# Sixteen experts of unequal load on one core: tiles of one or two experts replaced by tiles of up to four, in equal column strips

## The chip, the cores and the metric

The kernel runs on one core of a Trainium2 chip. The metric is the device time of one execution in microseconds (us); lower is better. Engines are named as in the profile: PE (TensorE, with PEld for its weight loads), DVE (VectorE), ACT (ScalarE), POOL (GpSimd) and SP (SyncE, which here issues the weight loads).

## What is computed

A two-layer backbone over 256 latent and 256 context tokens of width 1024. Each layer first mixes tokens in four branches (a recurrence, a long convolution, a short convolution, attention), merges them and normalises; none of that is touched. Then follows a mixture of 16 experts of which every token uses two. Layer 0 routes all 512 tokens, layer 1 the 256 latent ones:

```python
def moe(h, router_w, router_bias, w1, w3, w2):
    ...
    wts = jnp.take_along_axis(s, idx, axis=-1)
    wts = wts / jnp.sum(wts, -1, keepdims=True)
    gates = jnp.einsum('nk,nke->ne', wts, jax.nn.one_hot(idx, N_EXPERTS, dtype=F32)).astype(h.dtype)
    out = jnp.zeros_like(hf)
    for e in range(N_EXPERTS):
        act = jax.nn.silu(hf @ w1[e]) * (hf @ w3[e])
        out = out + gates[:, e:e + 1] * (act @ w2[e])
    return out.reshape(B, T, D)
```

Per expert w1 and w3 are 1024 x 512 and w2 is 512 x 1024, all fp32: 2 MB each, 6 MB an expert, 96 MB a layer.

## The kernel before

**Places and tiles.** The function `moe` routes, counts the tokens of each expert, and sorts the experts by count into 16 places; place 0 and place 1 always hold experts 0 and 1, so that their weights can be loaded before routing is known. A tile is 128 rows, one row for each token-expert pair, and `ROOM` says how many rows a place owns. `WORK` lists groups as (first place, experts, tiles). A group is one expert in one, two or three tiles of its own, or two neighbouring experts that share one tile, 64 columns each.

**One group.** `expert_in` (L1413) multiplies the tile's 128 gathered tokens by w1 and w3: the tokens are the stationary operand, w1 and w3 move through, 8 blocks of 128 rows each. Where two experts share a tile, each has 64 columns of the stationary operand, so that its output stands on its own 64 partitions. ACT and DVE form silu(.) times the other half (L1425), PE transposes that (L1429), and `expert_out` (L1445) multiplies by w2, whose result ACT writes out to `yd`. For the next group, PE finds the token numbers with 128x1 matmuls (L1543), the tokens are gathered by DMA, and PE turns them (L1560); layer 1 gathers by matmuls instead. `places` is the DVE operation that makes a tile's choice matrix.

**Weights.** A load is half of one matrix, 1 MB, 4 of its 8 row blocks for w1 and w3, 2 of 4 for w2. All 96 loads of a layer go out in order on SP's queue: those of experts 0 and 1 from L371, the others from L1691 with an expert number that SP has read first (L1702). They fill a ring of 11 buffers in layer 0 and 13 in layer 1, so that load i is issued when the matmuls on load i-11 (or i-13) are done.

**Room that runs out.** Where an expert has more tokens than its rows, a loop at the end (`For_i`, L1724) takes 128 of them a turn, of one expert, with loads of its own; `NOV` is the most turns that the layer may need, and the part of `yd` for them is set to zero at the program's start by DMAs from POOL (L1788).

**Counts.** The reference's routing of its drawn inputs gives, by place, in layer 0: 68 51 260 169 87 71 64 56 34 31 28 27 25 20 19 14 tokens; in layer 1: 46 38 65 55 44 41 32 30 28 26 23 22 18 17 16 11.

Of the kernel before, what the change touches and what calls it, by code (L numbers as in the profile page):

```python
# [34 lines left out]

ROOM = ([128, 128, 384, 256, 128, 128] + [64] * 10, [64, 64, 128, 128] + [64] * 12)
# [30 lines left out]
def host_constants():  # L67

    f = np.float32
    cols = {}  # L70
# [62 lines left out]
    for l in range(DEPTH):  # L133
        cols[f"room{l}"] = np.broadcast_to(np.array(ROOM[l], f), (128, 16))
        cols[f"base{l}"] = np.broadcast_to((np.cumsum(ROOM[l]) - ROOM[l]).astype(f), (128, 16))
    early = ("win", "zT", "iota", "lead", "token", "room0", "base0", "room1", "base1")
# [29 lines left out]
def backbone(ctx: ExitStack, tc: tile.TileContext, a: dict, out: bass.AP, dbg=None):  # L166
# [1234 lines left out]

    def expert_in(xs, w1, w3, n):


        W = 128 // n
# [29 lines left out]

    def expert_out(aa, w2, n, ydst):

        W = 128 // n
        py = [[xbank(), xbank()] for _ in aa]
        for k in range(4):  # L1440
            for h in range(2):
                for x in range(n):
                    c = slice(W * x, W * x + W)
                    for p, t in zip(py, aa):
                        PE.matmul(p[h][c, :], t[:, k, c], w2[x](k)[:, h * 512:h * 512 + 512], start=(k == 0),  # L1445
                                  stop=(k == 3), skip_group_check=n > 1)
        for p, d in zip(py, ydst):
            aas["y"] = aas.get("y", 0) + 1
            yo = wt("y1", [128, 1024]) if aas["y"] % 2 else unit("R7")[:, :1024]
            for h in range(2):  # L1450
                ACT.activation(yo[:, h * 512:h * 512 + 512], p[h], AF.Copy)  # L1451
            ACT.dma_start(d, yo)

    def moe(l, hh, hl, s, nt, crit, closing):
# [70 lines left out]
        DVE.scalar_tensor_tensor(qp, qv, 1.0, oh, op0=OP.add, op1=OP.mult)  # L1525
        work = WORK[l]
        xu = [0, None, 0]
# [26 lines left out]
        def turned(t, dst):  # L1554
# [7 lines left out]
            return dst  # L1562

        def chosen_rows(g, queue):
            p0, n, tiles = work[g]
            out = []
            if xu[2] % 2:
                xu[2] += 1
            for j in range(tiles):
                P = wt("y0", [128, 1024])[:, j % 2 * 512:j % 2 * 512 + nt * 128]  # L1570
                P = P.rearrange("p (i t) -> p i t", i=nt)
                qj = queue[:, :, p0:p0 + n]
                if j:
                    qj = wt("m_rq", [128, 2, 4, 2], bufs=1)[:, 0, :nt, :1]
                    DVE.tensor_scalar(qj, queue[:, :, p0:p0 + 1], -128.0 * j, None, op0=OP.add)
                marks.append(places(P, iota, qj, nt, n, 128 // n).ins)
                out.append(rows_of(P))
            return out

        def inputs(g, queue):  # L1580

            p0, n, tiles = work[g]
            out = []
            for j, dst in enumerate(room_for(tiles)):
                P = wt("y0", [128, 1024], F32R)[:, j % 2 * 512:j % 2 * 512 + nt * 128]
                P = P.rearrange("p (i t) -> p i t", i=nt)
                qj = queue[:, :, p0:p0 + n]
                if j:
                    qj = wt("m_rq", [128, 2, 4, 2], bufs=1)[:, 0, :nt, :1]
                    DVE.tensor_scalar(qj, queue[:, :, p0:p0 + 1], -128.0 * j, None, op0=OP.add)  # L1590
                marks.append(places(P, iota, qj, nt, n, 128 // n).ins)
                out.append(gather(P, hh, hl, dst))
            return out

        marks = list(crit)
        direct = nt == 2
        if direct:
            xs = inputs(0, qp)
        else:
            xs = [turned(t, d) for t, d in zip(chosen_rows(0, qp), room_for(work[0][2]))]  # L1600
        first = list(marks)
# [93 lines left out]
        def fetch(w, es):  # L1695

            hs = [[half(w, e, x) for e in es] for x in range(2)]
            per = D * DE // a[w].shape[3] // 256
            return [lambda k, j=j: hs[k // per][j](k) for j in range(len(es))]
# [4 lines left out]
        starts = [sum(ROOM[l][:p]) for p in range(16)]  # L1704
        for g, (p0, n, tiles) in enumerate(work):
            es = [p if p < 2 else expert(p) for p in range(p0, p0 + n)]
            queue = qs if g + 1 < len(work) and work[g + 1][0] > 1 else qp
            if not direct and g + 1 < len(work):
                rows = chosen_rows(g + 1, queue)
            with ExitStack() as order:  # L1710
                if g == 0:
                    for mk in first:
                        order.enter_context(tc.issue_after(mk))
                aa = expert_in(xs, fetch("exp_w1", es), fetch("exp_w3", es), n)
            if g + 1 < len(work):
                if direct:
                    xs = inputs(g + 1, queue)
                else:
                    xs = [turned(t, d) for t, d in zip(rows, room_for(work[g + 1][2]))]
            expert_out(aa, fetch("exp_w2", es), n,  # L1720
                       [yd[starts[p0] + 128 * j:starts[p0] + 128 * j + 128, :] for j in range(tiles)])
        closing()

        with tc.For_i(0, nc.values_load(ni[0:1, 0:1], min_val=0, max_val=NOV[l]), 1) as jv:  # L1724
            ev = SP.value_load(exi[0:1, ds(jv + 16, 1)], min_val=0, max_val=NE - 1)
            rg["tags"], rg["n"] = ("R0", "R1", "R9", "TZ", "R2", "cv0"), 0
            ws = [fetch(w, [ev]) for w in ("exp_w1", "exp_w3", "exp_w2")]
            P = wt("y0", [128, 1024], F32R if direct else F32)[:, :nt * 128].rearrange("p (i t) -> p i t", i=nt)
# [6 lines left out]
            dst = room_for(1)[0]  # L1735
            aa = expert_in([gather(P, hh, hl, dst) if direct else turned(rows_of(P), dst)], ws[0], ws[1], 1)
            expert_out(aa, ws[2], 1, [yd[ds(jv * 128 + XB, 128), :]])
        rg["tags"], rg["n"] = ("ring",), 0
# [222 lines left out]
```

## Time and profile before

| | |
|---|---|
| median of three runs | 1873.0 us (1869.58 to 1877.13) |
| the profiled execution's own time | 1867.61 us |
| its span | 1865.5 us |
| PE busy | 1665.6 us, 89% of the span |
| DVE, ACT, POOL busy | 46%, 30%, 6% |
| mean DMA rate | 206 GB/s over the span |
| experts of layer 0 on PE | 729.0 to 1075.9 us |
| experts of layer 1 on PE | 1579.4 to 1829.7 us |

The span is the time from the first to the last instruction; the execution's own time lies 2.1 us above it. PE's share is an average over the whole program. The two expert stages, which the change touches, are read apart from the rest, in windows and in the timeline.

### The profile page before, as it was taken

Reading aid. Unit: us, or ns where it says so; the run is one execution under the profiler, and the core shown is the slowest. Engines: PE = TensorE matmul, PEld = TensorE weight load, DVE = VectorE, ACT = ScalarE, POOL = GpSimd, SP = SyncE. Lnnn points to the kernel's source line nnn. Section 1 sums busy time; section 2 is a strip of 40 time slices with the busy share of each in tenths; the row PEclk is TensorE's granted clock in tenths of the full one; section 3 lists DMA queues with packets and bytes.
Section 4 is the critical chain, followed back from the end, with each engine's and each line's share of the span. In section 5 each row is a group of like instructions: output and inputs, shape, how many; then the busy total and the mean of one; then the engine's idle time right before and its main releaser. Section 6 shows DMA issues by size and latency. Waiting matters only on the chain. (4 is left out here: it accounts for less than half of the span.)

```text
span 1865.5 us, 24828 instructions
## 1 busy us (share of the span) xinstructions
PE 1665.6 (89%) x9699; PEld 1103.5 (59%) x9699; DVE 859.9 (46%) x1934; ACT 561.9 (30%) x1031; POOL 117.7 (6%) x160
## 2 busy tenths in 40 slices
PE   4999999999999987999999929989999996999982
PEld 2667766777778875444444306667888985444430
DVE  4464457777444585101010066576887677000002
ACT  2253144553223411111111144544654352111101
POOL 5100000000000010000000030000000001000001
PEclk8999999999999986999999969989999996999996
DMA  9614452112233355873979954266222466979993
GB/s 358 236 46 166 150 203 103 52 63 77 75 119 119 124 223 187 296 310 134 372 273 374 403 202 158 69 226 216 89 77 87 135 216 242 376 287 420 420 421 147
DMA packets 123350, 384.84 MB, mean 206 GB/s; under 512 B 8790, under 2 KB 75102, under 8 KB 92382
## 3 DMA queue, kind: packets, MB, share of 16 engines
q1 hardware_dynamic: 106176, 329.41, 47.2%
q10 hardware_dynamic: 10238, 33.23, 4.8%
q0 software_dynamic: 6816, 20.58, 3.2%
q8 instruction: 78, 1.28, 0.3%
q14 instruction: 42, 0.34, 0.1%
HBM read 361.62 MB, written 21.56 MB: 205 GB/s over the span
## 5 line engine op out<-in xcount | busy, mean ns | idle before, releaser
L355 PE MATMUL acc<-hA,cv 128*128 128x512 f32 (+1 forms) x864 | 308.5, 357 | 7.3 <-ACT hA L614 3.9
L356 PE MATMUL acc<-hA,cv 128*128 128x512 f32 (+1 forms) x864 | 306.7, 356 | 1.2 <-DVE cv L327 1.2
L357 PE MATMUL acc<-hB,cv 128*128 128x512 f32 (+1 forms) x864 | 304.5, 353 | 0.0
L355 PEld LDWEIGHTS acc<-hA,cv 128*128 128x128 f32 x864 | 164.2, 190 | 51.4 <-issue 15.8
L357 PEld LDWEIGHTS acc<-hB,cv 128*128 128x128 f32 x864 | 164.3, 190 | 28.8 <-issue 8.2
L356 PEld LDWEIGHTS acc<-hA,cv 128*128 128x128 f32 x864 | 164.6, 191 | 26.7 <-issue 3.5
L327 DVE TENSOR_TENSOR cv<-ring,cv 128x1024 fp32r<-128x1024 f32 (+1 forms) x108 | 126.9, 1180 | 32.2 <-ACT cv L326 32.0
L1425 DVE TENSOR_TENSOR y<-XS,k 128x512 f32<-128x512 f32 x15 | 15.4, 1029 | 267.7 <-PE k L1413 267.0
L326 ACT ACTIVATE cv<-ring 128x1024 fp32r<-128x1024 f32 (+1 forms) x108 | 109.0, 1020 | 19.9 <-DMA ring<-in_w_in_dram 14.4
L1413 PE MATMUL k<-R,R 128*64 128x512 f32 (+1 forms) x288 | 108.4, 599 | 3.0 <-DMA R<-in_exp_w_dram 3.0
L394 PE MATMUL ada<-ring,csf 128*32 128x512 f32 x336 | 62.3, 664 | 13.7 <-ACT csf L230 10.1
L1413 PEld LDWEIGHTS k<-R,R 128*64 128x64 f32 (+1 forms) x288 | 36.7, 152 | 56.5 <-issue 50.7
L1333 ACT ACTIVATE gt<-acc 128x512 f32<-128x512 f32 (+1 forms) x64 | 31.3, 490 | 114.5 <-PE acc L357 108.7
L1413 PE MATMUL acc<-R,R 128*64 128x512 f32 (+1 forms) x160 | 60.3, 594 | 1.7 <-DMA R<-in_exp_w_dram 1.7
L1425 DVE TENSOR_TENSOR y<-XS,acc 128x512 f32<-128x512 f32 x7 | 7.2, 1028 | 114.6 <-PE acc L1413 114.6
L1342 DVE SCALAR_TENSOR_TENSOR gt<-gt,o 128x512 f32<-128x512 f32 (+1 forms) x48 | 26.5, 552 | 70.2 <-PE o L357 68.8
L1413 PE MATMUL k<-ring,R 128*64 128x512 f32 (+1 forms) x144 | 54.0, 606 | 0.0
L1545 DVE CAST m_ix<-o 128x1 int32<-128x1 f32 x14 | 2.2, 158 | 106.3 <-PE o L1543 106.3
L978 DVE TENSOR_TENSOR R<-R 128x32 f32<-128x32 f32 (+14 forms) x120 | 49.7, 414 | 2.6
L1445 PE MATMUL k<-R,y 128*64 128x512 f32 (+1 forms) x124 | 45.6, 593 | 0.8 <-DVE y L1430 0.8
L1561 ACT ACTIVATE R<-o 128x512 f32<-128x512 f32 x28 | 16.4, 596 | 97.0 <-PE o L1560 97.0
L355 PE MATMUL o<-R,R 128*128 128x512 f32 (+1 forms) x128 | 44.8, 350 | 0.0
(567 smaller groups left out, 3306.5 us busy)
## 6 DMA issues: line engine op xcount, KB each, us to landing
R<-in_exp_w_dram SPq DMA_DIRECT2D x87, 1024.0 KB
ring<-in_w_in_dram SPq DMA_DIRECT2D x51, 1024.0 KB
ring<-in_ada_w_dram SPq DMA_DIRECT2D x42, 1024.0 KB
ring<-in_exp_w_dram SPq DMA_DIRECT2D x34, 1024.0 KB
cv<-in_exp_w_dram SPq DMA_DIRECT2D x31, 1024.0 KB
hB<-in_exp_w_dram SPq DMA_DIRECT2D x24, 1024.0 KB
TZ<-in_exp_w_dram SPq DMA_DIRECT2D x16, 1024.0 KB
y<-in_w_branch_dram SPq DMA_DIRECT2D x32, 256.0 KB
```

The source lines that it names most:

```text
L326: first = ACT.activation(hi, src, AF.Copy)
L327: DVE.tensor_tensor(lo, src, hi.bitcast(F32), op=OP.subtract)
L355: PE.matmul(o, lh, rh, start=start, stop=False)
L356: PE.matmul(o, ll, rh, start=False, stop=False)
L357: PE.matmul(o, lh, rl, start=False, stop=stop)
L394: PE.matmul(po[32 * q:32 * q + 32, :], csf[:, 2 * k:2 * k + 32], t[:, 512 * q:512 * q + 512], start=(k == 0), stop=(k == 7), skip_group_ch ...
L978: DVE.tensor_tensor(P4[:, :, :, :i + 1], T4[:, :, :, :i + 1], row[:, None, :, :].to_broadcast([128, 8, 2, i + 1]), op=OP.mult)
L1333: ACT.activation(gt, gp, AF.Tanh, scale=0.5)
L1342: DVE.scalar_tensor_tensor(gt, gt, 1.0, q, op0=OP.add, op1=OP.mult)
L1413: PE.matmul(q[c, :], t[:, k, c], w[x](k), start=(k == 0), stop=(k == 7), skip_group_check=n > 1)
L1425: DVE.tensor_tensor(t.rearrange("p (k c) -> p c k", k=4), act.rearrange("p (c k) -> p c k", k=4), p3.rearrange("p (c k) -> p c k", k=4), o ...
L1445: PE.matmul(p[h][c, :], t[:, k, c], w2[x](k)[:, h * 512:h * 512 + 512], start=(k == 0), stop=(k == 3), skip_group_check=n > 1)
```

## The change

The diff replaces `WORK` by `PLAN`, which lists for each group its tiles and for each tile the places in it with their columns. Layer 0 has 7 groups and 10 tiles instead of 11 and 14, layer 1 has 6 groups of one tile instead of 9. `strips` cuts a tile into equal strips (one of 128 columns, two of 64 or four of 32), and a place wider than a strip owns several, each with its own matmul on the same weights. Within a group, `expert_in` now does four row blocks of one tile before the next tile (`expert_out` two); before, the tiles of a group alternated at every matmul.

```diff
-WORK = ([(0, 1, 1), (1, 1, 1), (14, 2, 1), (2, 1, 3), (12, 2, 1), (3, 1, 2), (10, 2, 1), (4, 1, 1), (5, 1, 1),
-         (8, 2, 1), (6, 2, 1)],
-        [(0, 2, 1), (2, 1, 1), (3, 1, 1)] + [(p, 2, 1) for p in range(4, 16, 2)])
-XB = max(sum(r) for r in ROOM)
-NOV = (10, 5)
+PLAN = ([[[(0, 128)]],
+         [[(8, 64), (9, 32), (10, 32)]],
+         [[(2, 128)], [(2, 128)], [(2, 32), (5, 96)]],
+         [[(1, 64), (7, 64)]],
+         [[(4, 96), (14, 32)]],
+         [[(3, 128)], [(3, 64), (6, 64)]],
+         [[(11, 32), (12, 32), (13, 32), (15, 32)]]],
+        [[[(0, 64), (1, 64)]],
+         [[(2, 96), (15, 32)]],
+         [[(3, 64), (4, 64)]],
+         [[(5, 64), (6, 32), (7, 32)]],
+         [[(8, 32), (9, 32), (10, 32), (11, 32)]],
+         [[(12, 32), (13, 32), (14, 64)]]])
...
+NOV = (14, 10)
...
+    def strips(t):
+
+        n = min(w & -w for _, w in t)
+        return [(p, 32 * c, n) for c, p in zip(range(0, 4, n // 32), [p for p, w in t for _ in range(w // n)])]
...
-            for k in range(8):
-                for x in range(n):
-                    c = slice(W * x, W * x + W)
-                    for q, t in zip(qs, xs):
-                        PE.matmul(q[c, :], t[:, k, c], w[x](k), start=(k == 0), stop=(k == 7),
-                                  skip_group_check=n > 1)
+            for k4 in (0, 4):
+                for q, t, g in zip(qs, xs, group):
+                    for k in range(k4, k4 + 4):
+                        for p, c0, n in strips(g):
+                            c = slice(c0, c0 + n)
+                            PE.matmul(q[c, :], t[:, k, c], w[p](k), start=(k == 0), stop=(k == 7),
+                                      skip_group_check=n < 128)
...
-        iota = M2(128)
-        ex = M2(160).rearrange("p (n e) -> p n e", e=16)
+        iota = wt("Wn", [128, 128], bufs=2)
+        ex = M2(240).rearrange("p (n e) -> p n e", e=16)
...
-        for g, (p0, n, tiles) in enumerate(work):
-            es = [p if p < 2 else expert(p) for p in range(p0, p0 + n)]
...
+        for g, group in enumerate(work):
+            ps_ = sorted({p for t in group for p, _ in t})
+            es = {p: p if p < 2 else expert(p) for p in ps_}
```

The rooms that follow from `PLAN` are, by place, 128 64 288 192 96 96 64 64 64 32 and 32 for the rest in layer 0, and 64 64 96 64 64 64, seven of 32, 32, 64 and 32 in layer 1. `choices` makes a tile's matrix with one `places` operation for each run of places of equal width, where there was one for a tile. `NOV` grows, so that 28 DMAs of 256 KB instead of 20 set `yd` to zero.

SP's queue of before, at the end of layer 0's loads that need no routing (`m_exi` is the table of expert numbers, read with one TENSOR_LOAD each):

```order
L371 DMA hB_837_5579<-in_exp_w_dram 128x2048
L371 DMA cv_838_5581<-in_exp_w_dram 128x2048
L371 DMA cv_839_5583<-in_exp_w_dram 128x2048
L371 DMA R_840_5585<-in_exp_w_dram 128x2048
L371 DMA R_849_5628<-in_exp_w_dram 128x2048
L1702 TENSOR_LOAD m_exi_5435
L1702 ISA x2
L1702 TENSOR_LOAD m_exi_5435
L1702 ISA x2
```

Ten such reads follow one another before the ring's next load. The same place in the changed kernel:

```order
L400 DMA TZ_5562<-in_exp_w_dram 128x2048
L1739 TENSOR_LOAD m_exi_5444
L1739 ISA x2
L1739 TENSOR_LOAD m_exi_5444
L1739 ISA x2
L1739 TENSOR_LOAD m_exi_5444
L1739 ISA x2
L1728 ISA
L1728 DMA hB_847_5642<-in_exp_w_dram 128x2048
L1728 ISA
L1728 DMA cv_848_5644<-in_exp_w_dram 128x2048
```

Expert 1 has moved to the fourth group, so six loads instead of twelve need no routing, and three reads stand before the first load that does.

PE in the group of place 2, first products with w1, before (k, ada and acc are the three tiles' PSUM banks):

```order
L1413 MATMUL k_5883<-R_901_5852,R_880_5760 128x512
L1413 MATMUL ada_5884<-R_901_5852,R_880_5760 128x512
L1413 MATMUL acc_5885<-R_901_5852,R_881_5761 128x512
L1413 MATMUL k_5883<-R_901_5852,R_880_5760 128x512
L1413 MATMUL ada_5884<-R_901_5852,R_880_5760 128x512
L1413 MATMUL acc_5885<-R_901_5852,R_881_5761 128x512
```

and in the changed kernel (R_885 holds the weights of place 2, R_886 those of place 5):

```order
L1447 MATMUL acc_5876<-R_885_5860,R_864_5742 128x512 x4
L1447 MATMUL k_5877<-R_885_5860,R_864_5742 128x512 x4
L1447 MATMUL ada_5878<-R_885_5860,R_865_5743 32x512
L1447 MATMUL ada_5878<-R_886_5862,R_865_5743 32x512 x3
L1447 MATMUL ada_5878<-R_885_5860,R_865_5743 32x512
L1447 MATMUL ada_5878<-R_886_5862,R_865_5743 32x512 x3
```

The last two rows come four times: the third tile is now four strips, one of place 2 and three of place 5, and the width of the strips changes twice in each half of a matrix.

PE in the last group of layer 0, changed kernel only (before it was two strips of 64):

```order
L1447 MATMUL k_6665<-hB_1017_6633,R_1004_6540 32x512
L1447 MATMUL k_6665<-cv_1018_6635,R_1004_6540 32x512
L1447 MATMUL k_6665<-cv_1019_6637,R_1004_6540 32x512
L1447 MATMUL k_6665<-R_1020_6639,R_1004_6540 32x512
L1447 MATMUL k_6665<-hB_1017_6633,R_1004_6540 32x512
```

Each row block now needs four loads at once, one of each expert.

## Rows read from the trace of the kernel before

**Rows 1.** Windows, both expert stages: engines' busy time, PE clock, DMA share, rate.
```profile
core 0: us, PE busy (x) PEld busy (x) DVE busy (x) ACT busy (x) POOL busy (x), PEclk, DMA share, GB/s
729.00:1076.00 347.00, 329.98 (x1169) 144.73 (x1169) 37.41 (x79) 40.87 (x68) 15.19 (x14) 0.99 0.79 305
...
1579.40:1829.70 250.30, 232.63 (x1061) 103.12 (x1060) 20.46 (x37) 26.98 (x44) 0.00 (x0) 0.97 0.92 371
```
**Rows 2.** PE's waits, 715 to 1080 us: for what, total us, times, longest.
```profile
PE o L1429 <- DVE y L1425: 13.3, 12, 1.6
```
**Rows 3.** PE's waits for weights, 1555 to 1850 us.
```profile
PE k L1413 <- DMA R<-in_exp_w_dram: 3.0, 2, 1.7
PE acc L1413 <- DMA R<-in_exp_w_dram: 1.7, 1, 1.7
```
**Rows 4.** Window in the middle of layer 1's experts, and its DMA queues (packets, MB, share).
```profile
1665.00:1815.00 150.00, 137.92 (x704) 58.80 (x702) 10.30 (x14) 15.54 (x26) 0.00 (x0) 1.00 1.01 419
...
q1 hardware_dynamic: 8175, 59.57, 95.8%
q10 hardware_dynamic: 864, 3.15, 5.1%
```
**Rows 5.** Timeline of PE, layer 0's experts: start, us, operation.
```profile
729.01 8.83 PE L1413 MATMUL k<-ring,R 128*128 128x512 f32 x16
...
952.90 0.64 PE L1413 MATMUL k<-R,R 128*64 128x512 f32 x1
...
978.38 3.68 PE L1413 MATMUL ada<-TZ,R 128*128 128x512 f32 x8
...
1003.17 7.11 PE L1413 MATMUL acc<-ring,R 128*128 128x512 f32 x16
...
1052.14 3.60 PE L1413 MATMUL ada<-cv,R 128*64 128x512 f32 x16
...
1075.26 0.59 PE L1445 MATMUL k<-cv,y 128*64 128x512 f32 x1
...
1109.82 0.47 PE L675 MATMUL k<-cst,R 128*128 128x128 f32 x1 [33.97 <-DVE R L666]
```
**Rows 6.** Timeline of PE, two strips of 64 columns side by side.
```profile
1028.50 0.59 PE L1413 MATMUL k<-hB,R 128*64 128x512 f32 x1
1028.51 0.59 PE L1413 MATMUL k<-cv,R 128*64 128x512 f32 x1
```
**Rows 7.** Timeline of PE, four strips of 32 columns in another part (L394).
```profile
34.65 1.07 PE L394 MATMUL ada<-hB,csf 128*32 128x512 f32 x8
35.54 1.04 PE L394 MATMUL ada<-R,csf 128*32 128x512 f32 x8
```
**Rows 8.** Timeline of PE where the strips' width changes.
```profile
780.36 1.07 PE L1413 MATMUL acc<-ring,R 128*64 128x512 f32 x2
781.38 1.04 PE L1543 MATMUL o<-Wn,y 128*128 128x1 f32 x8
```
**Rows 9.** Windows: the group of three tiles, and layer 0's last five groups.
```profile
811.80:878.00 66.20, 65.45 (x174) 30.18 (x174) 5.69 (x8) 5.38 (x9) 1.14 (x1) 1.00 0.41 151
953.00:1076.00 123.00, 114.26 (x460) 46.82 (x460) 11.03 (x17) 13.14 (x22) 4.36 (x4) 1.00 0.98 390
```
**Rows 10.** Timeline of DVE: the expert numbers, layer 0.
```profile
725.49 0.17 DVE L1619 CAST m_exi<-Sf 128x16 int32<-128x16 f32 x1
```
**Rows 11.** Timeline of SP's queue: loads at the start of both expert stages.
```profile
734.44 0.34 SPq L371 DMA_DIRECT2D ring<-in_exp_w_dram  x1
...
1576.90 8.02 SPq L1691 DMA_DIRECT2D R<-in_exp_w_dram  x2
```
**Rows 12.** POOL: zeroing DMAs by line, and its next awaited work in the timeline.
```profile
L1788 POOL DMA_DIRECT2D yd<-XS x20 | 11.0, 555 | 13.4 <-DMA yd<-XS 10.9 <-DMA R<-in_rwkv_w_up_dram 1.1 <-DMA R<-in_hyena_w_dram 0.7
...
129.27 0.73 POOL L781 TENSOR_SCALAR R<-R 128x512 f32<-128x512 f32 x1 [69.44 <-ACT R L780]
```
**Rows 13.** Page, costliest groups: one row of token numbers for each tile of layer 0.
```profile
L1545 DVE CAST m_ix<-o 128x1 int32<-128x1 f32 x14 | 2.2, 158 | 106.3 <-PE o L1543 106.3
```

More of the change, by code (lines that the diff above doesn't have):

```diff
@@ L1434, in backbone, with expert_out @@
     aas = {"n": 0}
-    def expert_out(aa, w2, n, ydst):
-        W = 128 // n
+    def expert_out(aa, w2, group, ydst):
         py = [[xbank(), xbank()] for _ in aa]
[L1440 to L1446, printed above, removed]
+        for k2 in (0, 2):
+            for o, t, g in zip(py, aa, group):
+                for k in (k2, k2 + 1):
+                    for h in range(2):
+                        for p, c0, n in strips(g):
+                            c = slice(c0, c0 + n)
+                            PE.matmul(o[h][c, :], t[:, k, c], w2[p](k)[:, h * 512:h * 512 + 512], start=(k == 0),
+                                      stop=(k == 3), skip_group_check=n < 128)
         for p, d in zip(py, ydst):
@@ L1562, in turned, with choices @@
             return dst
+        def choices(g, queue, dt):
+            seen = {}
+            for j, t in enumerate(work[g]):
+                P = wt("y0", [128, 1024], dt)[:, j % 2 * 512:j % 2 * 512 + nt * 128]
+                P = P.rearrange("p (i t) -> p i t", i=nt)
+                c, x = 0, 0
+                while x < len(t):
+                    p, w = t[x]
+                    n = 1
+                    if not seen.get(p):
+                        while x + n < len(t) and t[x + n] == (p + n, w) and not seen.get(p + n):
+                            n += 1
+                    qj = queue[:, :, p:p + n]
+                    if seen.get(p):
+                        qj = wt("m_rq", [128, 2, 4, 2], bufs=1)[:, 0, :nt, :1]
+                        DVE.tensor_scalar(qj, queue[:, :, p:p + 1], float(-seen[p]), None, op0=OP.add)
+                    marks.append(places(P[:, :, c:c + n * w], iota, qj, nt, n, w).ins)
+                    for y in range(n):
+                        seen[p + y] = seen.get(p + y, 0) + w
+                    c, x = c + n * w, x + n
+                assert c == 128
+                yield P
@@ L1564, in chosen_rows @@
         def chosen_rows(g, queue):
-            p0, n, tiles = work[g]
-            out = []
             if xu[2] % 2:
                 xu[2] += 1
[L1569 to L1577, printed above, removed]
@@ L1578, in chosen_rows @@
-            return out
-        def inputs(g, queue):
[L1582 to L1593, printed above, removed]
+            return [rows_of(P) for P in choices(g, queue, F32)]
@@ L1595, in moe @@
+        def inputs(g, queue):
+            return [gather(P, hh, hl, dst) for P, dst in zip(choices(g, queue, F32R), room_for(len(work[g])))]
         marks = list(crit)
@@ L1599, in moe @@
         else:
-            xs = [turned(t, d) for t, d in zip(chosen_rows(0, qp), room_for(work[0][2]))]
+            xs = [turned(t, d) for t, d in zip(chosen_rows(0, qp), room_for(len(work[0])))]
         first = list(marks)
@@ L1695, in fetch @@
         def fetch(w, es):
-            hs = [[half(w, e, x) for e in es] for x in range(2)]
+            hs = [{p: half(w, e, x) for p, e in es.items()} for x in range(2)]
             per = D * DE // a[w].shape[3] // 256
-            return [lambda k, j=j: hs[k // per][j](k) for j in range(len(es))]
+            return {p: lambda k, p=p: hs[k // per][p](k) for p in es}
         def expert(x, most=NE - 1):
             return SP.value_load(exi[0:1, x:x + 1], min_val=0, max_val=most)
-        starts = [sum(ROOM[l][:p]) for p in range(16)]
-        for g, (p0, n, tiles) in enumerate(work):
-            es = [p if p < 2 else expert(p) for p in range(p0, p0 + n)]
-            queue = qs if g + 1 < len(work) and work[g + 1][0] > 1 else qp
+        for g, group in enumerate(work):
+            ps_ = sorted({p for t in group for p, _ in t})
+            es = {p: p if p < 2 else expert(p) for p in ps_}
+            queue = qs if g + 1 < len(work) and max(p for t in work[g + 1] for p, _ in t) > 1 else qp
             if not direct and g + 1 < len(work):
@@ L1718, in moe @@
                 else:
-                    xs = [turned(t, d) for t, d in zip(rows, room_for(work[g + 1][2]))]
-            expert_out(aa, fetch("exp_w2", es), n,
-                       [yd[starts[p0] + 128 * j:starts[p0] + 128 * j + 128, :] for j in range(tiles)])
+                    xs = [turned(t, d) for t, d in zip(rows, room_for(len(work[g + 1])))]
+            expert_out(aa, fetch("exp_w2", es), group,
+                       [yd[FIRST[l][g] + 128 * j:FIRST[l][g] + 128 * j + 128, :] for j in range(len(group))])
         closing()
@@ L1726, in moe @@
             rg["tags"], rg["n"] = ("R0", "R1", "R9", "TZ", "R2", "cv0"), 0
-            ws = [fetch(w, [ev]) for w in ("exp_w1", "exp_w3", "exp_w2")]
+            ws = [fetch(w, {0: ev}) for w in ("exp_w1", "exp_w3", "exp_w2")]
+            one = [[(0, 128)]]
             P = wt("y0", [128, 1024], F32R if direct else F32)[:, :nt * 128].rearrange("p (i t) -> p i t", i=nt)
```

30 lines of the change are left out of this document (22 added, 8 removed).

## The prediction

> **What bounds the kernel now.** I read the two expert stages in windows first [rows 1]. In layer 0 PE is busy 330 of 347 us with the DMA engines at 0.79: PE bounds it. In layer 1 PE is busy 233 of 250 us, but the DMA share is 0.92, so both are near. Next, what PE waits for. In layer 0 the largest wait is 13.3 us in twelve pieces, for DVE between the two products of a group [rows 2]; no weight is waited for. In layer 1 some waits are for weights, 3.0 and 1.7 us the largest [rows 3]. The window of 1665 to 1815 us shows why: a DMA share of 1.01 at 419 GB/s, and of that 59.57 MB were weight loads [rows 4]. So there the loads had caught up with PE: fewer tiles buy nothing beyond the time of the loads.
>
> One price comes from that window. 59.57 MB are 56.8 loads of 1.0486 MB; over 150 us a load takes 2.64 us, outputs included. At 419 GB/s with nothing else it would be 2.50 us. I take 2.64.
>
> The timeline of PE gives the price of a tile [rows 5]. A full tile's 16 records (8 row blocks, two passes each) take 7.11 us, 0.44 us a pass. One group of one tile runs from 978.38 to 1003.17: 24.8 us. Layer 0 begins at 729.0, its last five groups at 952.9, its last one at 1052.1, and its last product ends at 75.26 + 0.59 = 1075.9. The next PE work comes 34 us later, after DVE; that tail moves with the end.
>
> **The change, layer 0.** What does a tile in strips cost? Two strips of 64 begin 0.01 us apart [rows 6], and sixteen records of such pairs (four row blocks) take 3.60 us [rows 5], half of the full tile's time for half the row blocks. Four strips of 32 stand elsewhere in the kernel: eight records, four strips in two passes, begin 0.89 us before the next eight [rows 7]; a full-width row block has 2 x 0.44 = 0.88. So I cost a tile at a tile however it is cut. The Trainium skill, "TensorE: Matmul & The Clock Gate", section on packing small matmuls, measured three column strips of 32 at 2.38 times the speed of one after the other, not three times. By that a tile of narrow strips would be 26% dearer, and rows 7 do not bear it out here.
>
> The first six groups of the new plan have 1, 1, 3, 1, 1 and 2 tiles; the first six of the old have 1, 1, 1, 3, 1 and 2. The sum is the same, so on PE the seventh begins where the old seventh did, at 952.9. One thing is new: within two groups the strips' width changes, twice in each half matrix, six halves each: 24 changes. Where full-width work follows a pair of strips, the pair takes 781.38 - 780.36 = 1.02 us instead of 0.88 [rows 8], so 0.14 us a change, 3.4 in all (bounds 0, and 24 x 0.6 = 14 if a change cost a whole strip's record). The seventh group begins at 956.3. The Trainium skill, "TensorEngine Tiling (Array Packing)", key properties, says that changing the tiling mode drains the engine; it gives no price. It speaks against mixing widths, and the trace agrees with 0.14 us.
>
> From there one group replaces five. On PE alone it would be one tile of 24.8 us. But it has four experts: 24 loads, and the ring has 11 buffers. Load 84 goes out when the first four have been read, four row blocks after the start: 956.3 + 8 x 0.44 = 959.8. Then 13 loads follow at 2.64, 34.3 us, to 994.1. From the issue to the first byte I add 1.3 us (bounds 0 and one load's 2.6), and the last half matrix takes 3.6: the stage ends at 999.0. **Gain 1075.9 - 999.0 = 76.9 us.** At 2.50 a load it would be 78.7.
>
> This needs 83 loads in by 959.8. The first load that needs routing goes out after the expert numbers are cast at 725.49 + 0.17 [rows 10] and SP has read three of them. Before, ten reads lay between that and the load at 734.44 [rows 11], at most 0.88 each; three end at 728.3. The second group has three experts, and its last load is number 24: 728.3 + 18 x 2.64 = 775.8, about when PE reads it (that group ends near 780.4 less 3.6). I count no wait; up to 6 us is the bound. In the group of three tiles the DMA engines had only 0.41 of their time to do before, since the ring was full [rows 9]; in the new order that group is the third and reads 12 loads, so the ring is full again, some 11 ahead, near 846. From there 36 loads take 95 us, to 941. What holds 81 to 83 is then only when the sixth group's last matrices are read, just before 956. Behind it the last five groups ran at 390 GB/s [rows 9]: what was already nearly saturated becomes the limit.
>
> **Layer 1.** Every group now has two to four experts on one tile: 12 loads or more, at least 31.7 us, against about 26 of PE. So the loads bound the stage from start to end. The thirteen buffers let load 13 out as the second of two issues that begin at 1576.90 and end 8.02 us later, at 1584.9 [rows 11]. The other 83 take 83 x 2.64 = 219.1: 1804.0, with 1.3 and 3.6 the end is 1808.9. Before it was 1829.7. **Gain 20.8 us.** At 2.50 it would be 32.4. PE's six tiles at 26 us are 156 of these 224 us, so nothing that makes PE dearer by a third shows here.
>
> **Small things.** Eight more zeroing DMAs on POOL: 20 took 11.0 busy and 13.4 idle us, 1.2 each, so about 10 us more; POOL is next waited for at 129.27, after 69 us of idling [rows 12]: nothing (bound 5 if what POOL does at 57 us feeds something earlier than the view shows). The `iota` table moves to a shared buffer: its load comes long before routing, at most 0.5. More `places` operations on DVE lie beside 25 us of PE in each group: nothing; without that cover, about ten of them at under 1 us. Fewer outputs and gathers: counted in the 2.64.
>
> **Sum.** 76.9 + 20.8 = 97.7. The profiled execution took 1867.6; less 97.7 is 1769.9. It lies 5.4 us under the median of the runs, 1873.0. So 1775.3, **1775 us**. Its own range: cheaper loads take 13 off (1762); late weights in the second group and dear width changes add 6 + 11 (1792).
>
> **Rivals.**
> 1. *Weights later.* At the seventh group none of its 24 loads lies ahead, because something (a late second group, gathers beside the loads) has eaten the ring's lead. Then 24 x 2.64 = 63.4 from 956.3, plus 4.9: 1024.6, 25.6 later: about 1801. For it: 18 loads in the second group leave no slack. Against: the group of three tiles refills the ring.
> 2. *Narrow strips dearer.* If steps of four strips did not overlap, each would take its whole 1.07 us instead of 0.88 [rows 7]. A tile has 8 + 8 + 8 such steps, so three tiles of layer 0 before the last pay 72 x 0.19 = 14 us: 1789. (By the skill's 2.38 of 3 it would be 0.26 x 72 x 0.88 = 16 us, by an estimate from the page on the clock gate named above.) If only two of four ran side by side, a tile would cost 24 x 0.88 = 21 more: 63 in layer 0 and a few us in layer 1, about 1843. The starts in rows 7 speak against both; but there one load feeds all four strips, here up to four do.
> 3. *Better.* If the seventh group were not held by loads, layer 0 would gain 1075.9 - (952.9 + 23.7) = 99.3, and layer 1 32.4 at 2.50: 1741; half of that surplus, about 1755, is more likely.
> 4. *The other side: rooms overflow.* The new rooms are narrower: place 6 holds 64 tokens in 64 rows in layer 0 and 32 in 32 in layer 1. If a count ran over, a turn of the loop would follow, with one tile (24.8 us) and six loads that nothing prefetches (6 x 2.64 = 15.8): 40 us. Three turns cost 120, more than the gain: about 1895. It decides from the third turn on. Before, layer 0's page has 14 rows of token numbers, one for each planned tile [rows 13]: no turn was taken. By the counts of the reference none is now, unless the kernel's routing differs by a token where a place is exactly full.
>
> **How the numbers follow.** Forecast 0.60; weights later 0.15; narrow strips without overlap 0.10, two at a time 0.03; better 0.08; overflow 0.04. The range from 1758 to 1812 takes in the forecast's own range, later weights, and strips without overlap; it leaves out the two-at-a-time case, most of the overflow, and the better case. What a measurement of this kernel can tell from no change is about 0.5%, 9.4 us, the spread of its runs (7.6) being near that. All cases but overflow are faster by more; of the 0.04, one turn still gains, two come near nothing, three are slower: faster 0.95, same 0.02, slower 0.03.
>
> **What would show it.** Right: the seventh group of layer 0 starts near 956 and PE waits in it for weights, some 20 us; the stage ends near 999; in layer 1 the DMA share is near 1 from about 1503 (1580 less the gain of layer 0) to the end of the loads, and PE waits for weights in nearly every group; four strips of 32 begin within some hundredths of a us of each other, and a full step takes 0.89. Wrong: no waits in the seventh group (rival 3); waits in the second (rival 1); row blocks of 1.1 us or more in tiles of four strips (rival 2); more than ten rows of token numbers in layer 0 (rival 4). The forecast falls most easily where I count 11 loads ahead at one moment.

## The result

The median of four runs is 1794.7 us (1787.6 to 1804.1) against 1874.5: ratio 0.958, interval 0.9531 to 0.9629. A second set of six runs (e9) gave 0.962 (0.9596 to 0.9645). So the change gains some 71 to 80 us, and the forecast of 1775 was 20 too low, inside its range.

The profiled execution took 1787.6 us (span 1785.8), 80.0 less than that of before. Three windows of the changed kernel answer to [rows 1, 4, 9]: layer 0's experts, their last group, layer 1's experts.

```profile
core 0: us, PE busy (x) PEld busy (x) DVE busy (x) ACT busy (x) POOL busy (x), PEclk, DMA share, GB/s
737.90:1017.10 279.20, 258.73 (x1337) 96.23 (x1336) 28.05 (x68) 29.51 (x49) 10.50 (x11) 0.99 0.94 383
968.20:1017.10 48.90, 36.60 (x198) 8.73 (x196) 1.72 (x2) 1.79 (x3) 0.00 (x0) 0.93 0.98 398
1521.80:1747.70 225.90, 187.52 (x1145) 64.36 (x1144) 14.20 (x32) 18.01 (x29) 0.00 (x0) 0.93 0.97 402
```

Both stages now have a DMA share of 0.94 or more; in layer 1 PE is no longer busy throughout. From the timelines of PE (first and last product of each stage) the whole execution divides as follows, here for the kernels of this study too:

| kernel | layer 0 begins | layer 0, us | between, us | layer 1, us | after it, us |
|---|---|---|---|---|---|
| before | 729.0 | 346.8 | 503.6 | 250.2 | 35.8 |
| changed | 737.9 | 279.2 | 504.7 | 225.9 | 38.2 |
| changed, second time (e9) | 738.9 | 278.4 | 505.6 | 226.0 | 37.8 |
| e1, before with 28 zeroing DMAs | 740.6 | 349.0 | 507.5 | 249.7 | 35.8 |
| e2, zeroing partly later | 735.2 | 280.4 | 514.5 | 226.8 | 37.6 |
| e3, group of four earlier | 743.8 | 285.9 | 512.1 | 227.2 | 37.4 |
| e4, old tiles in layer 0 | 742.7 | 348.7 | 505.8 | 227.0 | 39.1 |
| e5, last group six loads | 740.4 | 260.0 | 512.8 | 262.5 | 39.0 |
| e6, tiles alternate | 739.0 | 297.6 | 507.2 | 227.1 | 37.5 |
| e7, zeroing at 140 us | 728.3 | 278.3 | 509.5 | 227.4 | 37.2 |
| e8, before, zeroing at 140 us | 730.3 | 346.6 | 508.1 | 246.2 | 35.2 |
| e10, no group of four | 739.2 | 278.2 | 506.5 | 227.1 | 38.0 |
| e11, e7 and e10 together | 728.5 | 280.3 | 503.8 | 227.0 | 37.4 |
| e12, e7 a second time | 730.3 | 282.2 | 505.5 | 227.1 | 37.6 |

Read from before to changed: the start costs 8.9 us, layer 0 gives 67.6, layer 1 gives 24.3, and the rest costs 3.5.

**The start.** This is what the prediction had at nothing. Rows, before and then changed, of the timelines of POOL, ACT (ACTq are the DMAs that it issues) and PE:

```profile
57.56 0.53 POOL L402 MEMSET gt<- 128x512 f32 x1
58.12 1.29 ACTq L404 DMA_DIRECT2D gt<-in_ada_b_dram  x4
59.45 0.60 ACT L1214 ACTIVATE R<-acc 128x512 f32<-128x512 f32 x1 [11.17 <-DMA gt<-in_ada_b_dram]
60.10 1.05 PE L1218 MATMUL o<-cst,R 128*128 128x2 f32 x8 [1.90 <-ACT R L1214]
...
70.10 1.80 PE L394 MATMUL ada<-ring,csf 128*32 128x512 f32 x8
```
```profile
62.35 0.54 POOL L431 MEMSET gt<- 128x512 f32 x1
62.93 0.90 ACTq L433 DMA_DIRECT2D gt<-in_ada_b_dram  x3
63.87 0.60 ACT L1243 ACTIVATE R<-acc 128x512 f32<-128x512 f32 x1 [14.34 <-DMA gt<-in_ada_b_dram]
64.52 1.86 PE L1247 MATMUL o<-cst,R 128*128 128x2 f32 x8 [5.49 <-ACT R L1243]
...
80.45 1.94 PE L423 MATMUL ada<-ring,csf 128*32 128x512 f32 x8
```

POOL's small memset of `gt` stands behind the zeroing DMAs, so it comes 4.8 us later. ACT's load of `ada_b` into `gt` waits for it, ACT's queue stands behind that load, and PE waits for ACT: 5.5 us of idling instead of 1.9. Then the granted clock falls. Two windows, before and changed:

```profile
66.00:72.00 6.00, 4.28 (x15) 1.18 (x15) 4.74 (x10) 2.98 (x6) 0.00 (x0) 0.86 0.44 161
78.00:84.00 6.00, 6.00 (x33) 4.20 (x32) 0.00 (x0) 1.65 (x3) 0.00 (x0) 1.00 0.60 195
```
```profile
66.00:72.00 6.00, 6.00 (x14) 1.46 (x14) 2.08 (x6) 0.00 (x0) 0.00 (x0) 0.50 0.45 180
78.00:84.00 6.00, 6.00 (x15) 1.99 (x15) 4.04 (x9) 0.00 (x0) 0.00 (x0) 0.52 0.49 169
```

After the longer idle the clock is at 0.50 and 0.52 in these windows, half speed (1.2 of 2.4 GHz), where before it was 0.86 and 1.00. By 80 us the changed kernel is 10 us behind: PE does at 80.45 what it did at 70.10.

**The last group of layer 0.** SP's queue and PE's timeline, changed kernel:

```profile
961.14 10.05 SPq L1728 DMA_DIRECT2D R<-in_exp_w_dram  x3
971.42 0.33 SPq L1728 DMA_DIRECT2D TZ<-in_exp_w_dram  x1
972.29 0.33 SPq L1728 DMA_DIRECT2D hB<-in_exp_w_dram  x1
...
977.19 1.04 PE L1447 MATMUL k<-R,R 128*32 128x512 f32 x2 [1.02 <-DMA R<-in_exp_w_dram]
979.70 1.04 PE L1447 MATMUL k<-TZ,R 128*32 128x512 f32 x2 [1.46 <-DMA TZ<-in_exp_w_dram]
982.20 1.06 PE L1447 MATMUL k<-hB,R 128*32 128x512 f32 x1 [1.46 <-DMA hB<-in_exp_w_dram]
```

The last of the three issues in the first row is load 82, at 970.85 (the row ends at 971.19, and an issue takes about 0.34); the next row is load 83, then 84 at 972.29. The group had begun at 968.26. So nine loads lay ahead of it, not eleven. PE then moves at the pace of the loads: a stall is some 1.46 us of waiting and 1.04 us in which one strip works alone, 2.50 us together. Waits for weights add up to only 10.8 us in this stage, where the prediction looked for some 20, although the group takes 48.8 instead of 24.8: the rest of the stall looks like busy time.

Windows show what came before: the end of the group of three tiles, the fourth to sixth group (with SP's own queue, which carries the loads: packets, MB, share), the seventh group's first 5 us, and most of the rest of it.

```profile
840.00:867.00 27.00, 26.24 (x142) 11.22 (x136) 2.87 (x5) 4.67 (x8) 0.00 (x0) 1.00 0.52 197
867.00:968.00 101.00, 97.13 (x504) 35.91 (x504) 9.35 (x17) 11.12 (x19) 4.02 (x4) 1.00 1.00 411
q1 hardware_dynamic: 5168, 37.67, 90.9%
968.30:973.00 4.70, 4.70 (x46) 1.41 (x48) 0.00 (x0) 0.60 (x1) 0.00 (x0) 1.00 0.69 237
973.00:1013.00 40.00, 28.18 (x136) 6.41 (x128) 1.72 (x2) 0.60 (x1) 0.00 (x0) 0.91 1.01 418
```

Until 867 us the ring is full (from 835 on SP waits 26.6 of 32 us for PE to free buffers), and the DMA engines have half their time free (0.52). From there to the seventh group they are busy throughout (1.00): 37.67 MB are 35.9 loads in 101 us, 2.81 us each with the gathers and outputs beside them. So from 867 us on it is the loads that decide when the stage ends, although PE waits for none of them before the last group, and the ring holds them up for a few us near 970 only. There SP's longest waits (from 960 to 985 us) are one for PE and one for an output to land, which ends just before load 82 goes out:

```profile
SPq L1728 <- PE acc L1479: 8.8, 1, 8.8
SPq L1728 <- DMA yd<-R: 8.6, 1, 8.6
```

Why a load waits for an output is not shown. Layer 1 shows the same pattern of stalls in the last three of its six groups. Two rows of PE's timeline there, one load (2.50 us) apart:

```profile
1654.96 1.04 PE L1447 MATMUL k<-hB,R 128*32 128x512 f32 x2 [1.44 <-DMA hB<-in_exp_w_dram]
1657.46 1.06 PE L1447 MATMUL k<-cv,R 128*32 128x512 f32 x1 [1.46 <-DMA cv<-in_exp_w_dram]
```

The first three groups do not wait for weights: the loads that went ahead cover them.

### The profile page after: what moved, and what is told of

Its sections match the earlier page's. It is cut to its first block, busy times and chain, and to the rows that moved or that the text cites. A ratio compares the mean times of both kernels' runs of the same rounds, so it can differ in the third digit from the quotient of the medians.

```text
span 1785.8 us, 25214 instructions
## 1 busy us (share of the span) xinstructions
PE 1553.8 (87%) x9943; PEld 1016.8 (57%) x9943; DVE 844.0 (47%) x1918; ACT 540.5 (30%) x996; POOL 116.4 (7%) x164
## 5 line engine op out<-in xcount | busy, mean ns | idle before, releaser
L356 DVE TENSOR_TENSOR cv<-ring,cv 128x1024 fp32r<-128x1024 f32 (+1 forms) x108 | 126.7, 1178 | 34.7 <-ACT cv L355 34.5
L1447 PE MATMUL k<-R,R 128*32 128x512 f32 (+2 forms) x392 | 111.1, 662 | 14.2 <-DMA R<-in_exp_w_dram 14.2
L1447 PEld LDWEIGHTS k<-R,R 128*32 128x32 f32 (+2 forms) x392 | 29.5, 132 | 71.6 <-issue 45.9
L1447 PE MATMUL k<-ring,R 128*32 128x512 f32 (+2 forms) x144 | 48.8, 690 | 2.8 <-DMA ring<-in_exp_w_dram 2.8
L1479 PE MATMUL k<-R,y 128*32 128x512 f32 (+2 forms) x160 | 47.6, 594 | 1.4 <-DVEq L1761 0.8
L384 PE MATMUL o<-R,R 128*128 128x512 f32 (+1 forms) x128 | 44.8, 350 | 0.0
L386 PE MATMUL o<-R,R 128*128 128x512 f32 (+1 forms) x128 | 44.4, 347 | 0.0
L1447 PE MATMUL acc<-R,R 128*32 128x512 f32 (+2 forms) x144 | 42.8, 629 | 1.5 <-DMA R<-in_exp_w_dram 1.5
L385 PE MATMUL o<-R,R 128*128 128x512 f32 (+1 forms) x128 | 43.9, 343 | 0.0
```

The costliest lines, as they stand in the source:

```text
L356: DVE.tensor_tensor(lo, src, hi.bitcast(F32), op=OP.subtract)
L384: PE.matmul(o, lh, rh, start=start, stop=False)
L385: PE.matmul(o, ll, rh, start=False, stop=False)
L386: PE.matmul(o, lh, rl, start=False, stop=stop)
L1447: PE.matmul(q[c, :], t[:, k, c], w[p](k), start=(k == 0), stop=(k == 7), skip_group_check=n < 128)
L1479: PE.matmul(o[h][c, :], t[:, k, c], w2[p](k)[:, h * 512:h * 512 + 512], start=(k == 0), stop=(k == 3), skip_group_check=n < 128)
```

## The experiments

Ratios are to the kernel before on the same chip. All kernels but e1, e4 and e8 have the new tiles in both layers.

**e1**: the kernel before with more zeroing.

```diff
-    yd = dr.tile([XB + 128 * max(NOV), D], F32, tag="yd", name="yd")
+    yd = dr.tile([XB + 128 * 14, D], F32, tag="yd", name="yd")
-            for j in range(max(NOV)):
+            for j in range(14):
```

> The kernel before with 28 zeroing DMAs instead of 20, nothing else. Theory (POOL's queue order: the second memset of gt stands behind the zeroing, ACT's load of ada_b waits for it, PE idles and its clock falls): PE's work from 80 us on is about 10 us later, the median 8 to 11 us above the kernel before, about 1884. Rival (the late start of the changed kernel comes from something else in the change, or from one execution): within 3 us of the kernel before.

Measured 1885.9 against 1870.4, ratio 1.0078 (1.0059 to 1.0097): the median is 15.5 us higher, more than the 8 to 11 expected. In its trace layer 0 begins 11.6 us later. So eight zeroing DMAs alone cost the kernel before what the table shows for the changed one, and a little more.

**e2**: the same 28 DMAs, written behind the branch that follows.

```diff
-        if l == 0:
-            z = wt("XS", [128, 4, 128]).rearrange("p a b -> p (a b)")
...
         ys[2] = sconv(l, lambda j: block(6 + j), n0)
+        if l == 0:
+            z = wt("XS", [128, 4, 128]).rearrange("p a b -> p (a b)")
...
```

> The changed kernel with the 28 zeroing DMAs issued later in POOL's queue, so that 11 stand ahead of the second memset of gt and 17 behind it; same bytes. Theory (queue order): the stall near 60 us goes, 9 to 14 us faster than the changed kernel's 1794.7, about 1783. Rival (the extra 2 MB delay the weight loads by their traffic, wherever they stand): less than 3 us faster.

Measured 1794.5, ratio 0.9584: no gain in the median. The theory was half right. In the trace the wait for `ada_b` is gone, and PE starts the same matmuls at 58.86 without idling. A few us later another wait stands there:

```profile
70.20 1.15 ACT L355 ACTIVATE cv<-ring 128x512 fp32r<-128x512 f32 x2 [4.88 <-DMA ring<-in_w_in_dram]
...
71.40 0.79 PE L384 MATMUL acc<-hA,cv 128*128 128x512 f32 x1 [6.71 <-DMA yd<-XS]
```

ACT now waits for a weight load, issued at 57.27, that shares the DMA engines with the zeroing (356 GB/s in this stretch, a share of 1.01). PE's row names a zeroing DMA as releaser; PE needs `cv`, which ACT and DVE make from that load. So both the queue order and the traffic count, and with the one gone the other takes over: layer 0 begins 2.7 us earlier instead of 9 to 14. In the traced execution that was lost again between the layers, which take 9.8 us more (514.5). The clock was 0.85 there from 1252 to 1275 us, which is worth some 3.5 us at most (0.15 of 23); what the others are is not shown.

**e7** and its repeat **e12**: all zeroing DMAs behind POOL's copy in the recurrence (L831), issued from 133.8 to 153.9 us in e7.

```diff
-            POOL.tensor_copy(N8, ident[:, None, :].to_broadcast([128, 8, 128]))
+            copied = POOL.tensor_copy(N8, ident[:, None, :].to_broadcast([128, 8, 128])).ins
+            if l == 0:
+                with tc.issue_after(copied):
+                    z = wt("XS", [128, 4, 128]).rearrange("p a b -> p (a b)")
...
```

> The changed kernel with all 28 zeroing DMAs behind POOL's copy at about 140 us, where POOL and the DMA engines have little to do. Theory now (both the queue order and the traffic of the zeroing delay the start): PE neither waits for ada_b nor for the weights near 60 to 72 us, the start is 10 us or more earlier than in the changed kernel, about 0.952 of the kernel before. Rival (the 7.3 MB delay whatever stands beside them): the 10 us come back after 140 us, 0.958.

> The changed kernel with the zeroing DMAs at about 140 us, once more, beside the changed kernel on the same chip. Theory (the late start is a cost of its own): 8 to 12 us faster than the changed kernel. Rival (the start's gain is lost again by the end): within 4 us.

Ratios 0.9558 (0.9533 to 0.9583) and 0.9549 (0.9526 to 0.9571). In the two traces layer 0 begins at 728.3 and 730.3, 8 to 10 us earlier than in the changed kernel, and the next long stretch is not delayed: a window of e7 from 142 to 172 us has PE busy for all 30 us at a clock of 1.00. So the late start is a cost of its own, and the zeroing is nearly free there.

How much of it reaches the end is less clear. e7's interval takes in the rival's 0.958 and not the expected 0.952. On the chip where the changed kernel ran beside it (e9), e12's median is 15.8 us lower (1784.6 against 1800.4), more than the 8 to 12 expected; the two traced executions, e9's fastest and e12's middle one, lie only 4.1 apart, since layer 0 took 3.8 us longer in e12. The plainest pair is e11 against e10 below, which differ in the zeroing alone: the start is 10.7 us earlier and the median 9.1 lower.

**e8**: the same move in the kernel before.

> The kernel before with its 20 zeroing DMAs behind POOL's copy at about 140 us. Theory: the kernel before loses a little to the same stall already (PE waits 1.9 and 1.7 us near 60 and 67 us and its clock falls to 0.86): 2 to 6 us faster, about 0.998. Rival (20 fit without harm): 1.000.

Ratio 0.9983 (0.9967 to 0.9999), as expected, but layer 0 begins 1.3 us later in its trace, not earlier. The trace does not show where the expected 2 to 6 us would come from: 20 zeroing DMAs do little harm.

**e4**: the old tiles written as a plan, layer 0 only.

```diff
-PLAN = ([[[(0, 128)]],
-         [[(8, 64), (9, 32), (10, 32)]],
...
+PLAN = ([[[(0, 128)]], [[(1, 128)]], [[(14, 64), (15, 64)]], [[(2, 128)]] * 3, [[(12, 64), (13, 64)]], [[(3, 128)]] * 2,
+         [[(10, 64), (11, 64)]], [[(4, 128)]], [[(5, 128)]], [[(8, 64), (9, 64)]], [[(6, 64), (7, 64)]]],
```

> The changed kernel with layer 0's old tiles (11 groups, 14 tiles) written as a plan, layer 1 as changed, 28 zeroing DMAs. Theory (terms add: start +9, layer 0 -68, layer 1 -21): 1874.5 + 9 - 21 = 1862. Rival (layer 1's gain depends on what layer 0 left behind, such as an earlier start of loads): more than 6 us away from 1862.

Measured 1864.9, on a chip where the kernel before took 1870.4 and e1 1885.9. Against e1, which has nearly the same start and layer 0, that is 21.0 us for layer 1. So layer 1's gain does not hang on what layer 0 left behind. The expected 1862 was worked out from 1874.5 and a start of 9 us; from this chip's 1870.4 it would be 1858.4. The 6.5 us between are the start, which cost 15.5 here (e1).

**e3**: the group of four experts directly behind the group of three tiles.

> The changed kernel with layer 0's group of four experts moved from the end to just behind the group of three tiles; the last group then has two experts. Theory (the last group is held by loads that the ring lets out late): the loads then run without a gap from about 870 us, the stage ends near 1001 instead of 1017, about 1780 us. Rival (layer 0 fell short because strips and their mixing with full-width work are dearer on PE): as many strips, so the same time within 4 us.

Measured 1799.1, ratio 0.9613 (0.9591 to 0.9636). The stage takes 285.9 us in the traced execution, the slowest of its five: 6.7 longer, not 15 shorter. The theory of the place fell: the group itself takes 49.5 us there as well, and the group behind it 35.5 instead of 25.2, since the loads are still late. From 876 to 1004 us the DMA share is 1.01, as it was near 1 in the changed kernel from 867 on: there was hardly a gap to close, and another order brings the same loads no sooner. The rival gave the right time, or nearly; that it is right about the cause is what e5 denies.

**e5**: the last group's four strips all use one expert's weights; the products with the other three are left out.

```diff
+            if lone:
+                hs = []
+                for x in range(2):
+                    t = half(w, next(iter(es.values())), x)
+                    hs.append({p: t for p in es})
```

> The changed kernel, but layer 0's last group multiplies all four strips by one expert's weights: 6 loads instead of 24, the other three experts' products are left out, PE does the same matmuls. Theory (the last group is held by loads that the ring of 11 lets out late): it takes 25 us instead of 48.8, 24 us faster than the changed kernel, 0.958 becomes about 0.945. Rival (four strips of 32 cost more on PE): still 45 us or more, within 4 us of the changed kernel.

In its trace the last group runs from 971.8 to 1000.4, 28.6 us instead of 48.8, with as many strips and matmuls:

```profile
971.80:1000.40 28.60, 24.40 (x198) 7.18 (x196) 4.08 (x4) 3.90 (x5) 0.00 (x0) 0.94 0.27 93
```

So 20 of the 24 us above a one-tile group belong to the loads; what the other 4 are is not shown. Leaving out 18 loads does not tell a late ring from full DMA engines; the windows of the last group above do. The whole run was slower all the same, 1811.3: other results of layer 0 gave layer 1 another routing, and one turn of the overflow loop ran at the end, from 1739.9 to 1775.7. That is 35.8 us, where the prediction had estimated 40. The run's median therefore says nothing on the theory; the group does.

**e6**: the old loop order, tiles alternating at each row block.

```diff
-            for k4 in (0, 4):
-                for q, t, g in zip(qs, xs, group):
-                    for k in range(k4, k4 + 4):
-                        for p, c0, n in strips(g):
...
+            for k in range(8):
+                for q, t, g in zip(qs, xs, group):
+                    for p, c0, n in strips(g):
...
```

> The changed plan with the old loop order: row block, tile, strips, so that the tiles of a group alternate at each row block. In the two groups that mix widths the width changes 96 times instead of 24. Theory (0.14 us a change): 72 changes more, 10 us, in those two groups; the stage ends about 10 us later, 0.958 becomes about 0.963. Rival (changes of width cost nothing, the loop order does not matter): the two groups within 2 us of the changed kernel's 67.9 and 45.9.

Measured 1816.6, ratio 0.9701 (0.9674 to 0.9728). Windows of the groups of place 2 and place 3, in e6 and then in the changed kernel:

```profile
800.20:875.40 75.20, 74.72 (x319) 23.08 (x318) 4.96 (x6) 5.97 (x10) 0.00 (x0) 1.00 0.68 275
932.10:987.10 55.00, 53.76 (x161) 14.56 (x160) 3.29 (x4) 4.78 (x8) 0.00 (x0) 1.00 0.85 341
```
```profile
799.00:866.90 67.90, 67.14 (x319) 26.40 (x318) 5.00 (x6) 7.05 (x12) 0.00 (x0) 1.00 0.78 313
922.30:968.30 46.00, 45.36 (x165) 16.65 (x166) 3.30 (x4) 4.78 (x8) 0.00 (x0) 1.00 1.00 409
```

They take 7.3 and 9.0 us more at the same clock: 16.3 us for 72 more changes of width, 0.23 each. Could it be the order of the tiles itself? e4 has the new order on full tiles alone. Its windows of the same two groups, and then those of the kernel before, which alternated:

```profile
828.30:894.40 66.10, 65.25 (x175) 30.46 (x174) 5.71 (x8) 6.46 (x11) 1.14 (x1) 1.00 0.42 157
923.40:968.40 45.00, 44.25 (x122) 20.85 (x121) 4.05 (x6) 4.78 (x8) 1.14 (x1) 1.00 0.61 236
```
```profile
811.80:878.00 66.20, 65.45 (x174) 30.18 (x174) 5.69 (x8) 5.38 (x9) 1.14 (x1) 1.00 0.41 151
907.10:952.90 45.80, 44.42 (x123) 20.72 (x122) 4.03 (x6) 4.71 (x8) 1.14 (x1) 1.00 0.60 232
```

Without a change of width the order is worth 0.1 and 0.8 us. So the changes cost something, more than worked out, and the new loop order saves them.

**e10** and **e11**: layer 0 without a group of four experts; e11 has the zeroing of e7 as well.

```diff
-         [[(1, 64), (7, 64)]],
-         [[(4, 96), (14, 32)]],
-         [[(3, 128)], [(3, 64), (6, 64)]],
-         [[(11, 32), (12, 32), (13, 32), (15, 32)]]],
+         [[(1, 64), (11, 32), (12, 32)]],
+         [[(3, 128)], [(3, 64), (6, 64)]],
+         [[(7, 64), (13, 32), (15, 32)]],
+         [[(4, 96), (14, 32)]]],
```

> The changed kernel with layer 0's groups arranged so that none has more than three experts and each group of 18 loads follows one of several tiles: (0), (8 9 10), (2 with 5), (1 11 12), (3 with 6), (7 13 15), (4 14); the same 10 tiles and 96 loads. Theory (loads bunch where a group needs more than the ring holds ahead): the waits for weights shrink, the stage ends about 10 us earlier, 0.953. Rival (any order pays the same, as moving the group of four did): within 3 us of the changed kernel.

> The groups without four experts and all zeroing DMAs at about 140 us together. Theory (the two costs are separate): 10 us from the stage and 10 from the start, 0.947 of the kernel before. Rival (what one gives the other takes back): no better than 0.952.

e10: 1790.1, ratio 0.9568 (0.955 to 0.9586), clear of e9's on the same chip. Its median has the expected 10 us, but its trace has layer 0 at 278.2 us, against 279.2 and 278.4 in the two traces of the changed kernel, and the waits for weights in it are 11.4 us against 10.8. From 870 to 1013 us its DMA share is 1.01. So by the traces the rival is right about layer 0: this order pays the same, and why the median is lower stays open. The two traces of the changed kernel are both of executions near the lower end of the changed kernel's runs (1787.6 to 1805.8), which spread more than those of e10 (1788.0 to 1794.3); what the others lose was not seen. e11: 1781.0, ratio 0.9525 (0.9508 to 0.9542), the fastest version here, 3.6 us under e12; the theory asked for 0.947, and the rival's 0.952 lies in the interval. What of e11 is the zeroing is shown; what the groups add is not.

**e9**: the changed kernel once more, beside e10 to e12.

> The changed kernel once more, to stand beside the next three on one chip: 0.958 of the kernel before, its start in the trace some 10 us later.

1800.4, ratio 0.962, layer 0 beginning at 738.9.

## Why the prediction was right, and where it missed

Of the 20 us by which the forecast was too low, layer 0 makes 9.3, the start 8.9, the rest of the program 3.5 and the spread of the runs 1.7; layer 1 gave 3.5 more than forecast.

**Layer 0, 76.9 forecast, 67.6 in the trace.** The mechanism was right: PE's six first groups take the same tiles as before, and one group replaces five, held by its loads. Two terms were too small. The first six groups take 230.4 us instead of the 223.9 of before plus 3.4. The group of three tiles accounts for 1.7, as its twelve changes at 0.14 say; that of two tiles shows 0.1. The second group takes 34.7 us, against 31.4 for the group before the three tiles in the old order, and the group before the two tiles is 1.1 longer too. In the second group, work for the next group's three tiles is put between the strips:

```profile
764.27 1.04 PE L1447 MATMUL ada<-hB,R 128*32 128x512 f32 x2
765.28 1.02 PE L1577 MATMUL o<-Wn,y 128*128 128x1 f32 x8
766.24 0.62 PE L1447 MATMUL ada<-hB,R 128*32 128x512 f32 x1
...
768.21 0.62 PE L1447 MATMUL ada<-hB,R 128*32 128x512 f32 x1
...
768.67 0.60 PE L1447 MATMUL ada<-cv,R 128*32 128x512 f32 x2
...
769.10 0.60 PE L1447 MATMUL ada<-cv,R 128*32 128x512 f32 x2
```

Full steps of four strips follow at 0.46 and 0.43 us a pass (768.21, 768.67, 769.10), as [rows 7] had it, so rival 2 is out. But where a full-width operation cuts a step, one strip runs alone and keeps PE for 1.01 us (764.27 to 765.28), as long as a whole step does before such an operation in [rows 8]. That price was not in the sum.

The last group was to take 42.7 us and took 48.8. The step that failed is "some 11 ahead", with loads 81 to 83 held "only" until the sixth group's last matrices are read. That end is where the seventh begins, so loads 82 and 83 joined the queue instead of lying ahead: 15 loads behind the start, not 13. Nor did the DMA engines have the 15 us to spare that the forecast left them, from 941 to 956. It had the ring full near 846, 117 us into the stage. The group of three tiles ended 129 us into it (866.9), mostly because the second group, which now prepares the three tiles, took 34.7 us and not the 24.8 of the old second one; and the next loads took 2.81 us each, not 2.64.

In the sum's terms: 15 loads take 38.8 us (2.5 for load 82, then 36.3 until the last is read at 1013.44) instead of 34.3 for 13, so 4.4 more. Load 82 is read 6.3 us after its issue (977.19), 3.8 more than a load at 2.50, where the forecast allowed 1.3 with a bound of 2.6. Its issue comes 2.6 us after the group's start, 0.9 before that of load 84 in the forecast. Together that is 6.0 of the 6.1 us. It is rival 1 in small.

**Layer 1, 20.8 forecast, 24.3 in the trace, 21.0 by e4 against e1.** Right in the end: the DMA share is 0.97 over the whole stage, and the loads run to about 5 us before its end (a share of 0.84 from 1740 to 1742 us, 0.24 in the two after). But PE waits in three of six groups, not in nearly every one, and is busy 187 of 226 us. By the forecast's own sum a load took 2.60 us, between the 2.64 taken and the 2.50 kept as a bound.

**The start, nothing forecast with a bound of 5, 8.9 in the trace.** This step of the prediction was wrong: "POOL is next waited for at 129.27". The view of POOL showed which wait of POOL came next, not which queue waits for POOL. The memset at 57.56 had no engine's compute behind it, only a DMA on ACT's queue. What releases that wait is written in ACT's row as a DMA, and so POOL's part in it was overlooked. e1 shows the cost by itself, e2 its two causes, and e7 and e12 that it goes when the zeroing is put elsewhere.

**The small rest.** Between the layers and after them the changed kernel's trace is 3.5 us longer. The median lies 7.1 us above the profiled execution, where before it was 5.4. In e2 and e3 the stretch between the layers is 7 to 10 us longer than here, with the clock at 0.83 to 0.85 from 1252 to 1275 us, where the changed kernel's trace has 1.00. The changed kernel's ten runs tend to have a lower mean clock the longer they take: 0.930 to 0.932 in the three under 1791 us, 0.926 or 0.927 in the five above 1799. So its slower runs lose clock somewhere; that it is there is not shown.

**The rules.** The Trainium skill's 2.38 for three narrow strips ("TensorE: Matmul & The Clock Gate", packing small matmuls) did not come out here for steps of four: 0.43 us a pass is that of a full-width pass. The drain at a change of tiling mode that the Trainium skill names ("TensorEngine Tiling (Array Packing)", key properties) did in part: 0.14 us a change in the group of three tiles, next to nothing in that of two, and 0.23 in e6.

**The rivals.** Overflow did not happen; its price of 40 us was near the 35.8 of e5. The better case needed the last group free of loads, which only e5 had.

## What to carry to other kernels

Where tiles are packed to save TensorE time, count the loads by group against the buffers that are free when the group begins: a buffer read by the last matmul of one group is not ahead of the next. Then look at how long the DMA engines have been full: where they are (here from 867 us to 1013, but for 5 us), another order of the groups brings the loads no sooner; in the traces of e3 and e10 it gained nothing. The time left free was before that, in the group of three tiles, where the ring was full; a ring of more buffers is not tried here. When DMAs are added to a queue, look for every memset and issue behind them and follow what waits for those, on the other engines' DMA queues too; and look at whose transfers share the engines then. A stage with many small waits can be bound by them even when their sum is small, since what runs between them (one strip of four) is counted as busy.

## What had not been expected of the hardware

A strip of 32 columns alone takes as long as four side by side: 0.86 us for two passes of 512 columns, as the last of the four strips shows in the last group of layer 0 (four together: 769.10 to 769.96 above).

```profile
1015.18 1.02 PE L1479 MATMUL acc<-cv,y 128*32 128x512 f32 x2
1016.04 1.02 PE L1479 MATMUL k<-cv,y 128*32 128x512 f32 x2
```

Idling near 60 us cost more than as much again afterwards: PE was 4.4 us late at 64.5 and 10.4 at 80.5, with 0.50 granted between. In e7 and e12, where PE idles 0.69 and 1.72 us between 63 and 67, the clock falls too, to 0.61 and 0.50 in the window of 66 to 72 us, but in that of 72 to 78 it is at 0.82 and 0.95, where the changed kernel still has 0.50. And DMAs of 256 KB on POOL's queue held up a 1 MB load from SP's queue: in e2, issued at 57.27, it was first read at 70.20, after a wait of 4.9 us; in e7, with no zeroing there, ACT read it, issued at 57.57, at 65.53 without one.
